# Attention output: the residual halves of the last two blocks are fetched ahead of the last four products

## The chip, the cores and the metric

One core of a Trainium2 chip runs the kernel in a single launch. The metric is device time in microseconds (us): 2112.7 us is the median of three runs before the change (2112.17 to 2113.65).

## The reference

The kernel computes a two-layer trunk on 1024 tokens of width 1024, in float32:

```python
for l in range(DEPTH):                       # DEPTH = 2
    if l < N_A:                              # layer 0
        h = h + recurrent_block(rmsnorm(h, a_norm[l]), ...)
    else:                                    # layer 1
        if l == N_A:
            k_pad, v_pad = shared_kv(h, kv_norm, w_kv, k_norm)
        q = rmsnorm((rmsnorm(h, b_norm[j]) @ b_w_q[j]).reshape(bsz, s, N_HEADS, HEAD_DIM), b_q_norm[j])
        o = chunk_band_attention(q, k_pad, v_pad, b_rel_bias[j])
        h = h + o @ b_w_o[j]                 # the change lies here
    h = h + sqrelu_mlp(rmsnorm(h, mlp_norm[l]), w_up[l], w_down[l])
```

`sqrelu_mlp(x) = square(relu(x @ w_up)) @ w_down`. The place of the change is `h + o @ b_w_o`: the product of the attention's output with its output weights, and the residual `h` that is added to it.

## The kernel before, in words

**Layout.** Activations lie transposed: 8 blocks of 128 features, each with 1024 tokens in two halves of 512 columns. Block `j`, half `h` is one tile of 128x512 floats (256 KB). A float32 product is made of three matmuls (L335 to L337, `mm`): each operand is split into a high part, copied by ScalarE in the reduced format, and a low part, the difference, made by VectorE. A product of one output tile has 8 blocks of input, so 24 matmuls of 512 columns.

**Attention output.** For output block `j` and half `h` TensorE sums the 24 matmuls in a PSUM bank. `Out.first` (L862) then fetches the residual tile from the DRAM tensor `x2d` into a buffer `s` of the pool `sp` (10 buffers, `sf()`), and VectorE adds bank and residual (L866) into `xr`. `Out.last` stores `xr` to the DRAM tensor `x3d`, since the MLP's last sum needs it again. Blocks 0 and 1 are made among the attention's own work. Blocks 2 to 5 are made by `Out.whole`, blocks 6 and 7 by `Out.end` in the order (6, 0), (7, 0), (6, 1), (7, 1), as (block, half).

**The MLP behind it.** The up product is one level of Strassen's scheme: seven products of sums of quarter matrices instead of eight. So the sums `xr` are themselves added, scaled by the norm's gains and split before TensorE can use them. For blocks 0 to 5 that is `Out.combine`, pair by pair. For blocks 6 and 7 it is the class `Begin`, which is written as chains of steps: `plain` and `mixed` wait for a flag `came[j, h]` that the residual sum sets, `square` and `lows` make the sum of squares for the norm, `sums` multiplies it with ones on TensorE (L366, L367), `outer` and `outer2` move the products out of PSUM (on ScalarE first: `c11`, `c22`), `loads` fetches the up weights of the second of 16 rounds. `mlp_up` then runs the rounds; in each the line L1356 makes the sum `c12` from a PSUM bank that TensorE's next product in that bank overwrites.

**What sets the order.** `end` and `Begin` stand in a region in which the program's own planner (`Plan`) steps the chains by estimated times and writes the instructions down in that order; each engine, and SyncE's queue, keeps it. Round 1 and later of `mlp_up` stand behind the region and are ordered by the framework's scheduler when the kernel is built. The same scheduler merges the region's first instructions with those of `whole` ahead of it. All DMAs here are issued by one engine, SyncE (SP), in order (`dma`, L244): one that has to wait holds those behind it.

Of the kernel before, what the change touches and what calls it, by code (L numbers as in the profile page):

```python
# [18 lines left out]
NF = 8  # L19
# [139 lines left out]
def tile_yoco_rglru_chunk_attention(  # L159
# [38 lines left out]
    def nm(s):  # L198
        cnt[0] += 1
        return f"{s}_{cnt[0]}"  # L200

    def gf(s="g"):
        return gp.tile([P, H2], F32, tag="g", name=nm(s))
# [4 lines left out]
    def sf(w=H2, s="s"):  # L208
        return sp.tile([P, w], F32, tag="s", name=nm(s))
# [22 lines left out]
    def bank(tag=None):  # L232
        if tag is None:
            tag = ("pj", "tp", "sc", "pj", "tp", "sc", "po", "sc")[ring[0] % 8]
            ring[0] += 1
        return ps1.tile([P, H2], F32, tag=tag, name=nm(tag), bufs=BANKS[tag])

    def hs(h):
        return slice(h * H2, (h + 1) * H2)
# [3 lines left out]
    def dma(dst, src):  # L243
        ins = nc.sync.dma_start(dst, src)  # L244
        if early[0]:
            early[0] -= 1
            tc.keep_in_program_order(ins)
# [91 lines left out]
    def mm3(ps, w, xs, half, span=None):  # L339
        n = len(xs)  # L340
        for k in range(n) if span is None else span:
            mm(ps, wparts(w, k), xs[k][half], k == 0, k == n - 1)
# [107 lines left out]
    def d_(n):  # L450
        return 0.16 + n * 0.00106
# [399 lines left out]
    class Out:  # L851
# [7 lines left out]
            self.XT = [[None] * 4 for _ in range(7)]  # L859
            self.rr = [None, None]  # L860

        def first(self, ps, j, h):  # L862
            xo = sf()
            dma(xo, self.resid[j, :, hs(h)])
            xt = gf("xr")
            dve.tensor_tensor(xt, ps, xo, ALU.add)  # L866
            self.XR[j][h] = xt
# [62 lines left out]
                    self.last(j, h)  # L930

        def end(self, Z, ws, plan, came):
            for h in range(2):
                for j in range(NF - 2, NF):
                    ps = bank()
                    for k in range(NF):
                        mm3(ps, ws[j], Z, h, (k,))
                        yield plan.pe(3 * H2) - LAT
                    self.first(ps, j, h)
                    came[j, h].set(plan.use("dve", d_(H2)))  # L940
                    self.last(j, h)

# [995 lines left out]
    for j in range(JP):  # L1938
        for h in range(2):
            ps = bank()  # L1940
# [80 lines left out]
```

## Time and profile before

| | before |
|---|---|
| median of three runs | 2112.7 us (2112.17 to 2113.65) |
| the profiled execution: run, span | 2111.56 us, 2109.8 us |
| granted TensorE clock, mean | 0.996 |
| TensorE busy | 2083.0 us (99%) |
| VectorE busy | 1564.0 us (74%) |
| ScalarE busy | 1104.0 us (52%) |
| GpSimd busy | 590.9 us (28%) |
| DMA | 319.19 MB, 151 GB/s in the mean |

The span runs from the first to the last instruction of the profiled execution; the run's time has some 1.8 us around it. In a row of the timeline the numbers are the start and the length in us; then engine, line of the kernel, operation, output `<-` inputs, shapes and count, and in brackets the engine's idle time before and what ended it. PE is TensorE, DVE VectorE, ACT ScalarE, POOL GpSimd, SPq SyncE's DMA queue. A row of waits reads: who waited for whom, total us, times, longest. The granted clock is the share of TensorE's full clock that was let through.

### The profile page before, as it was taken

To read this page: it belongs to the slowest core of one execution; us is meant where nothing else is said; L and a number is where in the kernel's file an instruction comes from. 1 tells how busy PE (TensorE), PEld (TensorE's weight loads), DVE (VectorE), ACT (ScalarE), POOL (GpSimd) and SP (SyncE) were. 2 spreads that over 40 slices of the span, in tenths; PEclk is the share of its full clock that TensorE was granted. 3 is DMA by queue.
4 is the path that set the end of the run, shared out by engine and by line. 5 is a ranking of instruction groups with operands and counts; after the bars stand their busy time and mean duration, and the time that the engine had idled before them with its cause. 6 is when DMAs were issued, how large, how long until landed. Compare 5 with 4: busy or idle time off the path is not lost.

```text
span 2109.8 us, 29361 instructions
## 1 busy us (share of the span) xinstructions
PE 2083.0 (99%) x9756; PEld 1729.7 (82%) x9756; DVE 1564.0 (74%) x2593; ACT 1104.0 (52%) x1965; POOL 590.9 (28%) x536
## 2 busy tenths in 40 slices
PE   9999999999999999999999999999899999999999
PEld 7788887888888888878888888878788888888887
DVE  8799869777777876557777777876877777777743
ACT  6878544344444454446666666764543434444631
POOL 2222104333300000047666666640233332000000
PEclk9999999999999999999999999999999999999999
DMA  4011436444488783523232233434444445987732
GB/s 163 30 51 58 160 101 209 150 154 149 156 316 278 229 256 118 160 83 100 81 94 86 77 88 99 121 119 133 158 162 150 150 151 193 327 260 245 237 107 93
DMA packets 174295, 319.19 MB, mean 151 GB/s; under 512 B 20544, under 2 KB 22592, under 8 KB 174144
## 3 DMA queue, kind: packets, MB, share of 16 engines
q1 hardware_dynamic: 174144, 317.33, 46.5%
q8 instruction: 76, 1.25, 0.3%
q14 instruction: 75, 0.61, 0.1%
HBM read 219.73 MB, written 78.64 MB: 141 GB/s over the span
## 4 chain that ended last, share of the span: by engine, by line
PE 91%; DVE 5%; DMA 1%; ACT 1%; issue 1%; SPq 0%; POOL 0%; DVEq 0%; ACTq 0%; POOLq 0%
PE pj L335 12%; PE pj L337 12%; PE pj L336 12%; PE tp L337 6%; PE tp L335 6%; PE tp L336 6%; PE sc L337 4%; PE sc L335 4%; PE sc L336 4%; PE p L336 4%; PE p L335 4%; PE p L337 4%; PE tp L1795 2%; PE po L1823 2%; PE po L1822 1%; PE sc L1770 1%
## 5 line engine op out<-in xcount | busy, mean ns | idle before, releaser
L335 PE MATMUL pj<-h,wh 128*128 128x512 f32 x1198 | 482.2, 403 | 3.4 <-DVE s L1356 2.4
L336 PE MATMUL pj<-l,wh 128*128 128x512 f32 x1198 | 468.7, 391 | 0.7 <-POOL l L1848 0.7
L337 PE MATMUL pj<-h,wl 128*128 128x512 f32 x1198 | 468.6, 391 | 0.0
L1066 ACT ACTIVATE wh<-raw 128x512 fp32r<-128x512 f32 x337 | 211.5, 630 | 325.1 <-PE po L336 82.7
L1067 DVE TENSOR_TENSOR wl<-raw,wh 128x512 fp32r<-128x512 f32 x337 | 270.0, 802 | 98.8 <-ACT wh L1066 94.9
L337 PEld LDWEIGHTS pj<-h,wl 128*128 128x128 f32 x1198 | 225.6, 188 | 48.9 <-DVE wl L1126 0.4
L335 PEld LDWEIGHTS pj<-h,wh 128*128 128x128 f32 x1198 | 226.3, 189 | 46.1 <-ACT wh L1066 2.6
L336 PEld LDWEIGHTS pj<-l,wh 128*128 128x128 f32 x1198 | 226.6, 189 | 39.5 <-POOL l L1848 1.4
L337 PE MATMUL tp<-h,wl 128*128 128x512 f32 x569 | 221.5, 389 | 1.4 <-DVE wl L1067 1.4
L335 PE MATMUL tp<-h,wh 128*128 128x512 f32 x569 | 221.5, 389 | 0.0
L336 PE MATMUL tp<-l,wh 128*128 128x512 f32 x569 | 221.4, 389 | 0.0
L349 DVE TENSOR_TENSOR l<-raw,h 128x512 fp32r<-128x512 f32 x224 | 153.5, 692 | 30.7 <-ACT h L348 29.4
L348 ACT ACTIVATE h<-raw 128x512 fp32r<-128x512 f32 x224 | 137.5, 620 | 55.4 <-DMA raw<-hid 32.6
L1327 ACT ACTIVATE s<-s 128x512 f32<-128x512 f32 x125 | 78.4, 629 | 166.4 <-DVE s L1326 166.3
L336 PE MATMUL sc<-l,wh 128*128 128x512 f32 x425 | 165.5, 389 | 0.0
L1075 POOL TENSOR_TENSOR raw<-raw,raw 128x512 f32<-128x512 f32 x30 | 49.9, 1664 | 412.4 <-DVE wl L1067 230.7
L337 PE MATMUL sc<-h,wl 128*128 128x512 f32 x425 | 165.2, 389 | 0.0
L335 PE MATMUL sc<-h,wh 128*128 128x512 f32 x425 | 165.2, 389 | 0.0
L335 PE MATMUL p<-h,wh 128*128 128x512 f32 x384 | 151.1, 394 | 1.6 <-ACT wh L493 1.5
L336 PE MATMUL p<-l,wh 128*128 128x512 f32 x384 | 150.3, 391 | 0.1
L337 PE MATMUL p<-h,wl 128*128 128x512 f32 x384 | 150.1, 391 | 0.0
L295 POOL TENSOR_TENSOR raw<-raw,vec 128x512 f32<-128x512 f32 x48 | 54.5, 1136 | 262.2 <-DMA raw<-in_w_kv 259.0
(302 smaller groups left out, 4235.8 us busy)
## 6 DMA issues: line engine op xcount, KB each, us to landing
raw<-hid SPq DMA_DIRECT2D x224, 256.0 KB, 3.6
hid<-s SPq DMA_DIRECT2D x221, 256.0 KB, 2.1
raw<-in_w_down SPq DMA_DIRECT2D x192, 256.0 KB, 3.5
raw<-in_w_up SPq DMA_DIRECT2D x128, 256.0 KB, 2.6
s<-in_w_down SPq DMA_DIRECT2D x64, 256.0 KB, 4.3
raw<-in_w_in SPq DMA_DIRECT2D x32, 256.0 KB, 2.7
raw<-in_w_kv SPq DMA_DIRECT2D x32, 256.0 KB, 3.4
od<-ev SPq DMA_DIRECT2D x48, 128.0 KB, 2.3
```

The lines of the kernel that those rows point to most:

```text
L295: pool.tensor_tensor(raw, raw, gains, ALU.mult)
L335: pe.matmul(ps, lhsT=wh, rhs=xh, start=start, stop=False, skip_group_check=more)
L336: pe.matmul(ps, lhsT=wh, rhs=xl, start=False, stop=False, skip_group_check=more)
L337: pe.matmul(ps, lhsT=wl, rhs=xh, start=False, stop=stop, skip_group_check=more)
L348: act.activation(h, src, AF.Copy)
L349: dve.tensor_tensor(l, src, h.bitcast(F32), ALU.subtract)
L1066: act.activation(wh, raw, AF.Copy)
L1067: dve.tensor_tensor(wl, raw, wh.bitcast(F32), ALU.subtract)
L1075: pool.tensor_tensor(raw[A11], raw[A11], raw[A21], ALU.add)
L1327: act.activation(out, out, AF.Square)
L1795: pe.transpose(pt[:, g * P : (g + 1) * P], sc[:, (kb - kb0) * P : (kb - kb0 + 1) * P], ident)
L1823: pe.matmul(out, lhsT=st, rhs=pl[:, off : off + wid], start=False, stop=y == final)
```

## The change

The four fetches of `Out.end` are issued at its start, in the order (6, 0), (7, 0), (6, 1), (7, 1), each into a buffer of its own; `first` takes the buffer when it is given one. Sums, stores and products are as they were.

```diff
-        def first(self, ps, j, h):
-            xo = sf()
-            dma(xo, self.resid[j, :, hs(h)])
+        def first(self, ps, j, h, xo=None):
+            if xo is None:
+                xo = sf()
+                dma(xo, self.resid[j, :, hs(h)])
             xt = gf("xr")
             dve.tensor_tensor(xt, ps, xo, ALU.add)
             self.XR[j][h] = xt
...
         def end(self, Z, ws, plan, came):
+            xo = {}
+            for h in range(2):
+                for j in range(NF - 2, NF):
+                    xo[j, h] = sf()
+                    dma(xo[j, h], self.resid[j, :, hs(h)])
             for h in range(2):
                 for j in range(NF - 2, NF):
                     ps = bank()
                     for k in range(NF):
                         mm3(ps, ws[j], Z, h, (k,))
                         yield plan.pe(3 * H2) - LAT
-                    self.first(ps, j, h)
+                    self.first(ps, j, h, xo[j, h])
                     came[j, h].set(plan.use("dve", d_(H2)))
                     self.last(j, h)
```

Six lines are added ahead of what follows, so the lines of `Begin` and `mlp_up` move by 6 (L1356 becomes L1362), the residual sum from L866 to L867.

The order moves at two places. On SyncE's queue, from the fetch of block 5's second half (`s_3736`) on, with the semaphores that each row waits for (those named DMAHW are of earlier DMAs on the same lane), before:

```order
L244 DMA s_3736_15208<-x2d_110 128x512 [waits DMAHW2_49]
L244 DMA x3d_111<-xr_3737_15210 128x512 [waits DMAHW3_49,DVE_49]
L244 DMA s_3764_15294<-x2d_110 128x512 [waits DMAHW4_49]
L244 DMA x3d_111<-xr_3765_15296 128x512 [waits DMAHW5_49,DVE_49]
L244 DMA s_3770_15331<-x2d_110 128x512 [waits DMAHW6_49]
L244 DMA x3d_111<-xr_3771_15333 128x512 [waits DMAHW7_49,DVE_49]
L244 DMA s_3775_15365<-x2d_110 128x512 [waits DMAHW0_49,Activation_49,Pool_49]
L244 DMA x3d_111<-xr_3776_15367 128x512 [waits DMAHW1_49,DVE_49]
L244 DMA s_3786_15410<-x2d_110 128x512 [waits DMAHW2_49,Activation_49]
L244 DMA x3d_111<-xr_3787_15412 128x512 [waits DMAHW3_49,DVE_49]
```

and with the change:

```order
L244 DMA s_3736_15208<-x2d_110 128x512 [waits DMAHW6_49]
L244 DMA x3d_111<-xr_3737_15210 128x512 [waits DMAHW7_49,DVE_49]
L244 DMA s_3759_15261<-x2d_110 128x512 [waits DMAHW0_49]
L244 DMA s_3760_15263<-x2d_110 128x512 [waits DMAHW1_49,Activation_49]
L244 DMA s_3761_15265<-x2d_110 128x512 [waits DMAHW2_49]
L244 DMA s_3762_15267<-x2d_110 128x512 [waits DMAHW3_49,Activation_49,Pool_49]
L244 DMA raw_3764_15273<-in_w_up 128x512 [waits DMAHW4_49]
L244 DMA raw_3765_15275<-in_w_up 128x512 [waits DMAHW5_49]
L244 DMA raw_3766_15277<-in_w_up 128x512 [waits DMAHW6_49]
L244 DMA raw_3767_15279<-in_w_up 128x512 [waits DMAHW7_49]
L244 DMA x3d_111<-xr_3768_15302 128x512 [waits DMAHW0_49,DVE_49]
L244 DMA x3d_111<-xr_3773_15337 128x512 [waits DMAHW1_49,DVE_49]
```

The stores (`x3d<-xr`) wait for VectorE's sum, and before the change a fetch stood behind each; now the four fetches stand together. The four loads of the second round's up weights (`in_w_up`), which stood among the fetches of blocks 3 to 5 before, now come behind them.

On VectorE, in the second round of the up product (the weight splits `wl`, and the sum of L1356), before:

```order
L1067 TENSOR_TENSOR wl_3843_15688<-raw_3760_15265,wh_3842_15687 128x512
L1067 TENSOR_TENSOR wl_3850_15733<-raw_3845_15724,wh_3849_15732 128x512
L1067 TENSOR_TENSOR wl_3852_15737<-raw_3846_15726,wh_3851_15736 128x512
L1067 TENSOR_TENSOR wl_3854_15741<-raw_3848_15730,wh_3853_15740 128x512
L1356 TENSOR_TENSOR s_3838_15679<-pj_3826_15584,s_3839_15680 128x512
L1067 TENSOR_TENSOR wl_3863_15805<-raw_3847_15728,wh_3862_15804 128x512
```

and with the change:

```order
L1073 TENSOR_TENSOR wl_3843_15688<-raw_3764_15273,wh_3842_15687 128x512
L1073 TENSOR_TENSOR wl_3850_15733<-raw_3845_15724,wh_3849_15732 128x512
L1073 TENSOR_TENSOR wl_3852_15737<-raw_3846_15726,wh_3851_15736 128x512
L1362 TENSOR_TENSOR s_3838_15679<-pj_3826_15584,s_3839_15680 128x512
L1073 TENSOR_TENSOR wl_3854_15741<-raw_3848_15730,wh_3853_15740 128x512
L1073 TENSOR_TENSOR wl_3863_15805<-raw_3847_15728,wh_3862_15804 128x512
```

The sum stands ahead of one weight split that it stood behind. TensorE's order is the same in both.

## The prediction

> **What bounds the kernel now.** I read the page's busy line first, then who TensorE waited for, then the chain of work that ended last around the place of the change.
>
> ```profile
> PE 2083.0 (99%) x9756; PEld 1729.7 (82%) x9756; DVE 1564.0 (74%) x2593; ACT 1104.0 (52%) x1965; POOL 590.9 (28%) x536
> ...
> PE po L366 <- ACT a L1122: 3.3, 1, 3.3
> ...
> PE pj L335 <- DVE s L1356: 2.4, 2, 2.2
> ...
> PE pj L335 <- DVE s L1362: 0.4, 1, 0.4
> ```
>
> The kernel is bound by TensorE (PE), busy 99% of the span. A wait row gives the total, the number of waits and the longest. The first lies just behind the four products of the change; the 2.2 of the second comes 30 us later. After 1530 us PE waits only 0.4 us (last row) to the end, so what is won before 1530 has nothing to hide behind. The chain says who sets the time between the two places (start, length, work):
>
> ```profile
> 1492.34 0.25 PE tp L337
> ...
> 1493.23 0.68 DVE wl L1126
> ...
> 1524.08 1.75 DVE wl L1067
> ...
> 1526.58 0.47 PE pj L335
> ```
>
> From 1492.6 to 1526.4 the path is VectorE (DVE), nearly without a gap; PE only joins again at 1526.58. DVE enters that stretch with the last residual sum. So the question is when that sum starts.
>
> ```profile
> 1479.10 0.69 DVE L352 SCALAR_TENSOR_TENSOR l<-s,h 128x512 fp32r<-128x512 f32 x1
> 1479.70 0.69 DVE L866 TENSOR_TENSOR xr<-tp,s 128x512 f32<-128x512 f32 x1
> 1481.24 0.75 DVE L1130 SCALAR_TENSOR_TENSOR l<-xr,vec,h 128x512 fp32r<-128x512 f32 x1 [0.85 <-ACT h L1122]
> 1481.91 0.69 DVE L1126 TENSOR_TENSOR acc<-acc,s 128x512 f32<-128x512 f32 x1
> 1484.08 0.69 DVE L866 TENSOR_TENSOR xr<-sc,s 128x512 f32<-128x512 f32 x1 [1.49 <-DMA s<-x2d]
> 1485.62 0.75 DVE L1130 SCALAR_TENSOR_TENSOR l<-xr,vec,h 128x512 fp32r<-128x512 f32 x1 [0.84 <-ACT h L1122]
> 1488.00 0.69 DVE L866 TENSOR_TENSOR xr<-po,s 128x512 f32<-128x512 f32 x1 [1.64 <-DMA s<-x2d]
> 1489.48 0.75 DVE L1130 SCALAR_TENSOR_TENSOR s<-xr,vec,s 128x512 f32<-128x512 f32 x1 [0.79 <-ACT s L1122]
> 1491.00 0.69 DVE L1126 TENSOR_TENSOR l<-s,h 128x512 fp32r<-128x512 f32 x1 [0.76 <-ACT h L1122]
> 1492.62 0.69 DVE L866 TENSOR_TENSOR xr<-sc,s 128x512 f32<-128x512 f32 x1 [0.93 <-PE tp L337]
> ```
>
> L866 is the residual sum; its four rows are (block 6, half 0), (7, 0), (6, 1), (7, 1). The brackets give idle time and releaser. The first sum follows other DVE work at once; the next two wait for the residual fetch. The last is put down to PE, but its product, the fourth of the four, was long done:
>
> ```profile
> 1484.01 0.39 PE L337 MATMUL sc<-h,wl 128*128 128x512 f32 x1
> ...
> 1480.42 0.32 SPq L244 DMA_DIRECT2D x3d<-xr  x1
> 1480.79 1.07 SPq L244 DMA_DIRECT2D s<-x2d  x1
> 1484.80 0.32 SPq L244 DMA_DIRECT2D x3d<-xr  x1
> 1485.22 0.37 SPq L244 DMA_DIRECT2D s<-x2d  x1
> ...
> 1489.13 0.38 SPq L244 DMA_DIRECT2D s<-x2d  x1
> ...
> DMA to landing us min/median/max: 2.0/2.7/5.7
> ```
>
> The fourth product ends at 1484.4, 8 us ahead of its sum. The fetch was issued at 1489.13, and about 3 us later (1492.6) it is there: the 0.93 is a DMA wait too. Each fetch stands on SyncE's (SP's) queue behind the store of the block before, and the store waits for that block's sum: sum, store, fetch, 3 us, sum.
>
> **The change part by part.** Nothing is computed anew: the same four fetches, sums and stores. (a) Three fetches leave the loop of sum, store and fetch. Before, (7,0) could be issued only behind the store at 1480.42. Now all four stand behind the store of block 5, and that one went out at 1470.88:
>
> ```profile
> 1470.88 0.32 SPq L244 DMA_DIRECT2D x3d<-xr  x1
> 1471.26 0.42 SPq L244 DMA_DIRECT2D s<-x2d  x1
> ```
>
> At 0.42 us each the last is issued at 1472.6. The worst landing above, 5.7 us, belongs to a burst of the stage before, so by the worst row all are there at 1478.3, ahead of the first sum (1479.70). What could hold them is their buffers. The fourth now waits for ScalarE and GpSimd, but in the program before the third fetch has the same two waits and went out at 1485.22, 0.1 us behind the store (1484.80 + 0.32): no price.
>
> The DVE steps then follow each other without DMA waits. Queued steps start 0.60 us apart (1479.10, 1479.70). Sum (7,0): 1481.91 + 0.60 = 1482.51. From a sum to the split behind it 1.54 (1484.08 to 1485.62): 1484.05. Sum (6,1), 0.67 behind (1481.24 to 1481.91): 1484.72. From there to the L1126 step 3.00 (1488.00 to 1491.00): 1487.72. Sum (7,1): 1488.32 in place of 1492.62. **4.30 us**, of which 4.06 are the three waits (1.49 + 1.64 + 0.93); the rest is queueing that overlaps. The fourth product (1484.4) is no limit.
>
> (b) PE's stall behind the products.
>
> ```profile
> 1492.18 0.40 PE L337 MATMUL tp<-h,wl 128*128 128x512 f32 x1
> 1495.89 0.50 PE L366 MATMUL po<-a,onesr 128*128 128x512 f32 x1 [3.31 <-ACT a L1122]
> 1497.03 0.79 PE L367 MATMUL po<-a,onesr 128*128 128x512 f32 x1 [0.65 <-DVE a L1126]
> 1498.02 0.80 PE L335 MATMUL pj<-h,wh 128*128 128x512 f32 x1 [0.20 <-ACT s L1122]
> ...
> 1500.61 0.39 PE L335 MATMUL pj<-h,wh 128*128 128x512 f32 x1
> 1500.84 0.39 PE L336 MATMUL pj<-l,wh 128*128 128x512 f32 x1
> ...
> 1497.00:1500.40 3.40, 3.17 (x7) 2.19 (x8) 3.40 (x6) 2.95 (x6) 0.00 (x0) 0.50 0.29 77
> ...
> 1527.80:1531.10 3.30, 3.30 (x9) 2.55 (x8) 3.15 (x4) 0.75 (x2) 1.13 (x1) 0.50 0.38 93
> ```
>
> The two rows by window end in granted clock, DMA share and GB/s. All that releases these three hangs on the last sum. 4.30 earlier, L366 is ready at 1491.59, so PE runs it as soon as it is free (1492.4); L367 at 1492.73; L335 at 1493.72. The stall shrinks to some 0.9 us and PE is 4.30 ahead. It also no longer enters a half clock (0.50): the six matmuls from 1498.02 to 1500.61 took 2.59 us; at 0.23 apart (1500.61 to 1500.84, the clock full again) they take 1.38, so 1.21 more. PE is then 5.51 ahead.
>
> (c) The next meeting point, 1526.58. PE's product there overwrites what the L1356 step reads. PE's last matmul before it starts at 1523.98; 5.51 earlier it is done at 1518.7. DVE's chain is 4.30 ahead, and one step has moved: the L1356 row now stands ahead of one weight split (the row at 1524.08, 1.67 us to the next start). 1525.75 - 4.30 - 1.67 = 1519.78; PE followed its start by 0.83: 1520.61. 1526.58 - 1520.61 = **5.97 us**. PE waits some 1.9 us there, as before (2.21), so the half clock behind it (1.65 of the 3.30 us at 0.50) stays.
>
> (d) One round later.
>
> ```profile
> 1525.75 0.68 DVE L1356 TENSOR_TENSOR s<-pj,s 128x512 f32<-128x512 f32 x1
> ...
> 1544.89 0.69 DVE L1356 TENSOR_TENSOR s<-pj,s 128x512 f32<-128x512 f32 x1 [0.37 <-issue]
> ...
> 1547.36 0.39 PE L335 MATMUL pj<-h,wh 128*128 128x512 f32 x1
> ...
> 1563.93 0.69 DVE L1356 TENSOR_TENSOR s<-pj,s 128x512 f32<-128x512 f32 x1 [0.94 <-PE pj L337]
> ```
>
> DVE could have been at the second L1356 at 1544.52; 4.30 earlier and 0.83 for PE gives 1541.05, 6.3 ahead of 1547.36. So no more than 6.3 passes here whatever PE wins before, and 5.97 passes. From the round after that on (1563.93) DVE waits for PE here, and the end follows PE.
>
> (e) The four loads of up weights in the same region now stand behind the fetches: issued by about 1474.4 (eight issues of 0.4 from 1471.26), landed by the worst row at 1480.1, and copied by ScalarE first here:
>
> ```profile
> 1501.04 0.63 ACT L1122 ACTIVATE wh<-raw 128x512 fp32r<-128x512 f32 x1
> ```
>
> 4.30 earlier that is 1496.7, so there are 16 us in hand. No price.
>
> The sum: 2109.8 - 6.0 = 2103.8 us of span. The run of that profile took 2111.56, the median of the runs shown is 2112.7, 1.14 more; I take 6.0 off the median: **2106.7 us**. Bounds: 4.3 if the moved step gives nothing; 6.3 by (d), beyond which up to 9.4 (5.51 + 2.21 + 1.65) if DVE's own stretch got shorter too.
>
> The half clock deserves care. Here waits of 2.21 and 3.31 us were followed by 0.50. The Trainium skill (TensorE: Matmul & The Clock Gate, "What's actually happening") says that the clock falls after an idle window of about 3.4 us. By that rule a wait of 1.9 us at 1518.7 would leave the clock full, and PE would be 5.97 + 1.65 ahead until (d) caps it: 2106.4. The trace speaks against it, since 2.21 sufficed; I keep 2106.7.
>
> **The rivals.** *The moved step gives nothing* (20%): L1362, as it is called now, waits for something else, or the splits ahead stretch. Then DVE's 4.30 is all: 2112.7 - 4.3 = 2108.4. For it: the chain there has steps of 1.5 to 1.75 where others take 0.60, so their length is not steady. Against it: the order is fixed at build.
>
> *More than the sum* (8%): DVE's stretch shortens as its steps meet GpSimd's otherwise, the second wait goes too. 2112.7 - 9.4 = 2103.3 at most.
>
> *Hidden* (12%): the sums find another wait, such as ScalarE's copies in line behind them (they take 0.8 each in the rows above), or DVE loses elsewhere what it gained, so that 0 to 3.5 is left: about 2111. Against it: the sums' only waits are fetch and product, and the products are done.
>
> *Slower* (5%): the up weights, now queued behind four fetches on SP, come late for the product after the stall. That decides only if they land after 1496.7, where ScalarE copies them; each us beyond costs PE one. To lose what is won they must land after 1502.7, 28 us behind their issue, against 5.7 as the worst of a fetch; at 33 us the time would be 2117. Only a buffer that comes free late could do it.
>
> **How the numbers follow.** The forecast case, 5 to 6.6 us, has 55%, the rivals 20, 8, 12 and 5. A measurement of this kernel tells about 0.2%, 4.2 us, from no change. Faster by over that: 55 + 8 + half of the 20, whose value lies on the line = 73%; within: 10 + 12 = 22%; slower 5%. For 8 in 10 I take 2104.5 to 2110.2: the forecast, the moved-step rival and a part of the next two. The likeliest case alone spans 2106.1 to 2107.7.
>
> **What would show it.** L867's waits for x2d gone in the last three sums, the last one near 1488.3; four x2d issues in a row behind 1470.9; L366's wait of 3.3 gone and no 0.50 clock at 1493 to 1497; PE's wait on L1362 (now c12's first sum) at 1519 to 1521. Wrong would be: a fetch issued late, or a last sum near 1488 with PE still resuming past 1524.

## The result and the profile after

The changed kernel takes **2101.86 us** (median of six runs, 2098.96 to 2102.58) beside 2112.7 us for the kernel before in six runs taken with them: a ratio of 0.9947, 95% interval 0.9934 to 0.9959. A second measurement of both programs gave 2102.53 beside 2110.78 us (ratio 0.9959, 0.9946 to 0.9971; five and 27 runs). The change is worth 8 to 11 us. I had forecast 6.0, and 2106.7 us; the time lies below the range.

The profiled execution of after took 2100.08 us, its span is 2098.3 us. First TensorE's busy line and its waits (total, times, longest), as they were shown of before:

```profile
PE 2077.5 (99%) x9756; PEld 1725.9 (82%) x9756; DVE 1559.2 (74%) x2593; ACT 1102.6 (53%) x1965; POOL 593.2 (28%) x536
...
PE pj L335 <- DVE s L1368: 1.5, 2, 1.1
...
PE pj L335 <- ACT s L1128: 0.5, 1, 0.5
PE pj L335 <- DVE s L1362: 0.4, 2, 0.3
```

The wait of 3.3 us behind the four products is down to 0.5, as forecast. But the wait of 2.2 us for the sum of round 1 (L1356 before, L1362 now), which I had left standing, is gone too. What is left on that line is 0.3 one round later (at 1535.77) and 0.2 in the first layer's MLP (at 350.89), which before has too. The two waits on L1368 have nothing to do with the change: 1.1 stands in the first layer's MLP at 603.86, where the kernel before with small GpSimd adds, shown below, has 0.9; and 0.4 stands at 1788, where the first profile of before has the same 0.4 (its L1362).

The timeline of after around the change: SyncE's queue, the four residual sums, and where TensorE resumes.

```profile
1468.40 0.32 SPq L244 DMA_DIRECT2D x3d<-xr  x1
1468.77 1.87 SPq L244 DMA_DIRECT2D s<-x2d  x4
1470.69 2.36 SPq L244 DMA_DIRECT2D raw<-in_w_up  x4
1477.93 0.33 SPq L244 DMA_DIRECT2D x3d<-xr  x1
...
1477.22 0.68 DVE L867 TENSOR_TENSOR xr<-tp,s 128x512 f32<-128x512 f32 x1
1480.03 0.69 DVE L867 TENSOR_TENSOR xr<-sc,s 128x512 f32<-128x512 f32 x1
1482.22 0.69 DVE L867 TENSOR_TENSOR xr<-po,s 128x512 f32<-128x512 f32 x1
1485.82 0.69 DVE L867 TENSOR_TENSOR xr<-sc,s 128x512 f32<-128x512 f32 x1
...
1491.22 0.50 PE L335 MATMUL pj<-h,wh 128*128 128x512 f32 x1 [0.49 <-ACT s L1128]
```

The four fetches go out together behind the store of block 5, no sum waits for one, and the last sum is 8.60 us behind the first (1485.82 - 1477.22) in place of 12.92 (1492.62 - 1479.70). That is 4.32 us won; the prediction had 4.30.

The two profiles differ by 2.5 us before the change is reached (the first sum is at 1477.22 against 1479.70). So all dates below are counted from a row that every program here has ahead of the place, TensorE's matmul that waits some 0.27 us for ScalarE at 1412.06 us before and at 1409.79 after (in us, "stretch" is VectorE's time from the last residual sum to the sum of round 1):

| from the row at 1412 / 1409 to | before | before, again | after | after, again |
|---|---|---|---|---|
| last residual sum | 80.56 | 80.54 | 76.03 | 75.88 |
| TensorE resumes behind the products | 85.96 | 85.95 | 81.43 | 81.28 |
| TensorE's product behind the sum of round 1 | 114.52 | 115.37 | 106.52 | 106.35 |
| the end of the span | 697.74 | 696.38 | 688.51 | 687.93 |
| VectorE's stretch | 33.13 | 34.01 | 28.89 | 28.89 |

At the end after is 8.8 us ahead (means of the two columns each). 4.6 us of it are there when TensorE resumes, the rest comes in the 30 us behind that: VectorE's stretch became 4.24 us shorter in the first pair and 5.12 in the second, where I had counted 1.67 for the step that changed its place. These rows show why. GpSimd adds weight quarters there (L1075 to L1080 before, L1081 to L1086 after); first before:

```profile
1503.86 2.27 POOL L1075 TENSOR_TENSOR raw<-raw,raw 128x512 f32<-128x512 f32 x1 [89.75 <-DMA s<-in_w_down]
1506.21 1.74 POOL L1076 TENSOR_TENSOR raw<-raw,raw 128x512 f32<-128x512 f32 x1
1506.72 1.79 DVE L1130 SCALAR_TENSOR_TENSOR rneg<-s,rneg 128x512 f32<-128x512 f32 x1
1511.44 2.38 DVE L1326 SCALAR_TENSOR_TENSOR s<-s,rneg 128x512 f32<-128x512 f32 x2
1511.65 1.62 POOL L1078 TENSOR_TENSOR raw<-raw,raw 128x512 f32<-128x512 f32 x1 [3.69 <-issue]
1513.74 1.77 DVE L1067 TENSOR_TENSOR wl<-raw,wh 128x512 fp32r<-128x512 f32 x1
...
1520.85 1.39 DVE L1067 TENSOR_TENSOR wl<-raw,wh 128x512 fp32r<-128x512 f32 x2
1522.32 1.29 POOL L1075 TENSOR_TENSOR raw<-raw,raw 128x512 f32<-128x512 f32 x1 [7.35 <-DVE wl L1067]
1522.55 3.28 DVE L1067 TENSOR_TENSOR wl<-raw,wh 128x512 fp32r<-128x512 f32 x2 [0.31 <-ACT wh L1066]
1523.68 1.59 POOL L1076 TENSOR_TENSOR raw<-raw,raw 128x512 f32<-128x512 f32 x1
```

and after:

```profile
1497.06 2.27 POOL L1081 TENSOR_TENSOR raw<-raw,raw 128x512 f32<-128x512 f32 x1 [85.23 <-DMA s<-in_w_down]
1499.41 2.33 POOL L1082 TENSOR_TENSOR raw<-raw,raw 128x512 f32<-128x512 f32 x1
1499.88 0.70 DVE L1136 SCALAR_TENSOR_TENSOR rneg<-s,rneg 128x512 f32<-128x512 f32 x1
...
1506.62 1.62 POOL L1086 TENSOR_TENSOR raw<-raw,raw 128x512 f32<-128x512 f32 x1
1507.24 1.56 DVE L1073 TENSOR_TENSOR wl<-raw,wh 128x512 fp32r<-128x512 f32 x1
...
1513.50 1.29 DVE L1073 TENSOR_TENSOR wl<-raw,wh 128x512 fp32r<-128x512 f32 x2 [0.50 <-ACT wh L1072]
1514.27 1.67 POOL L1081 TENSOR_TENSOR raw<-raw,raw 128x512 f32<-128x512 f32 x1 [6.03 <-DVE wl L1073]
1514.71 0.69 DVE L1362 TENSOR_TENSOR s<-pj,s 128x512 f32<-128x512 f32 x1
...
1516.31 0.39 PE L335 MATMUL pj<-h,wh 128*128 128x512 f32 x1
```

The same `rneg` step takes 1.79 us beside GpSimd's add before and 0.70 after, and there the add takes 2.33 in place of 1.74: in each of these pairs one of the two is held up by the other. The two splits ahead of L1356 took 3.28 us together, beside two adds; now the sum L1362 stands ahead of one of them, and the add at 1514.27 runs beside the sum, which reads PSUM and takes its 0.69. The sum is done before TensorE wants its bank, and TensorE runs into the product at 1516.31 with no wait. The Trainium skill (SBUF — State Buffer, "Who interferes with whom") says that a VectorE step with two SBUF inputs contends with a GpSimd step that reads SBUF, for a port pair that only one of them can hold, that the order of issue decides who is blocked, and that a VectorE step with at most one SBUF input, outside the two-port modes, does not contend; the rows above agree, with 1.56 to 1.79 against 0.70 us for the held steps and 0.69 for the sum out of PSUM.

### The profile page after: what moved, and what is told of

Same layout as the page of the kernel before. It is cut to its first block, busy times and chain, and to the rows that moved or that the text cites. A ratio compares the mean times of both kernels' runs of the same rounds, so it can differ in the third digit from the quotient of the medians.

```text
span 2098.3 us, 29355 instructions
## 1 busy us (share of the span) xinstructions
PE 2077.5 (99%) x9756; PEld 1725.9 (82%) x9756; DVE 1559.2 (74%) x2593; ACT 1102.6 (53%) x1965; POOL 593.2 (28%) x536
## 4 chain that ended last, share of the span: by engine, by line
PE 87%; DVE 6%; DMA 3%; issue 2%; ACT 2%; POOL 0%; SPq 0%; DVEq 0%; POOLq 0%; ACTq 0%
PE pj L335 11%; PE pj L336 11%; PE pj L337 11%; PE tp L337 6%; PE tp L335 6%; PE tp L336 6%; PE p L336 4%; PE p L337 4%; PE p L335 4%; PE sc L336 4%; PE sc L335 4%; PE sc L337 4%; PE tp L1801 2%; PE po L1829 2%; PE po L1828 1%
## 5 line engine op out<-in xcount | busy, mean ns | idle before, releaser
L1081 POOL TENSOR_TENSOR raw<-raw,raw 128x512 f32<-128x512 f32 x30 | 50.3, 1678 | 403.3 <-DVE wl L1073 226.2
```

Source lines behind the costliest of these rows:

```text
L1081: pool.tensor_tensor(raw[A11], raw[A11], raw[A21], ALU.add)
```

## The experiments

### Both programs once more

Copies with a comment added.

> The kernel before, once more, for the noise and for a second profile. 2.5 us of the 11.5 us between the two profiles lie ahead of the change (the sum of block 6 starts at 1479.70 before and 1477.22 after), some 1.7 of it in a bout of half clock at 1391 to 1394.7, behind a wait of TensorE of 1.9 us that both programs have. 'Chance': the bout belongs to the run, not to the kernel; this profile may show it or not, and the time stays within 2112.7 +- 1.5. 'The change did it': the bout and the 2.5 us are here again as in the kernel before, and not in the next run. Either way the wait of 3.3 us behind the four products and the one of 2.2 us in round 1 come back at the same offsets from the sum of block 6 (18.3 us and 46.9 us).

> The changed kernel, once more: 2101.9 +- 1.5 us. 'Chance' for the 2.5 us ahead of the change: this profile may have the half clock at 1391, and then the sum of block 6 is near 1479 and the time is up to 2.5 us longer than in the other runs. Both theories on the change: the last residual sum 8.6 us behind the first of the four (1485.82 - 1477.22), no wait of TensorE on the sum of round 1 over 0.5 us, no half clock behind the four products.

Measured: 2111.23 us (11 runs) and 2102.53 (5). The table above has the second profiles. The 2.5 us ahead of the change were chance: after, run again, has its first sum at 1479.95, as late as before, and without half clock near 1390, so that date moves by more than the one bout. In the first profile of before a half clock followed TensorE's wait of 1.90 us at 1389.93, in the second profile of before, with a wait of 1.98 us at the same place, it did not. The windows just behind that wait end in granted clock, DMA share and GB/s; first before, then before again:

```profile
1391.00:1394.40 3.40, 3.40 (x17) 3.17 (x16) 0.95 (x3) 2.11 (x5) 3.40 (x5) 0.53 0.00 0
```

```profile
1391.80:1395.20 3.40, 3.40 (x25) 3.05 (x25) 1.79 (x4) 2.84 (x7) 3.40 (x5) 1.00 0.00 0
...
1496.20:1499.60 3.40, 3.21 (x7) 2.22 (x8) 3.40 (x6) 2.95 (x6) 0.00 (x0) 0.50 0.28 77
1526.60:1529.90 3.30, 3.30 (x15) 2.74 (x16) 3.15 (x3) 1.27 (x2) 2.28 (x2) 1.00 0.24 75
```

The other two windows of before again stand behind the four products and behind the sum of round 1. The wait of 3.3 us brings half clock again, and for twice as long: the granted clock is at 0.50 from 1497.0 to 1500.4 in the first profile, 3.4 us, and from 1495.0 to 1501.9 in the second, 6.8 us. The wait of 1.94 us in round 1 does not this time, where 2.21 us did in the first profile. So the bout in round 1 that the prediction let "stay" is there in some executions of before and not in others, and the bout behind the products is there each time.

### The last residual sum late again

```diff
+                    if (j, h) == (NF - 1, 1):
+                        for _ in range(6):            # 3 in the second run
+                            dve.tensor_tensor(xo[j, h], xo[j, h], xo[j, h], ALU.max)
                     self.first(ps, j, h, xo[j, h])
```

All other instructions keep the order of after, on every engine.

> After, with six VectorE steps in place (each tile written over itself, values unchanged) ahead of the last residual sum, so that this sum is as late as before the change, by 6 x 0.60 to 0.75 = 3.6 to 4.5 us; the order of everything else is that of after. It separates the date of the last sum from the changed order in round 1. 'Chain' (time follows the last sum one to one): 2101.9 + 4.2 = 2106.1, or 2107.3 with the half clock behind TensorE's wait. 'Order and chain' (my prediction's sum): only the moved step of 1.67 stays won, 2112.7 - 1.7 = 2111.0. 'Meeting' (VectorE's stretch of 33 us is longer or shorter by how its steps meet GpSimd's, which start by other dates): anything up to 2112.7, with the wait on the sum of round 1 back at 0.5 to 2.2 us and VectorE's steps of 1.5 to 2.4 us among GpSimd's adds.

> After with three of the six VectorE steps ahead of the last residual sum, half the dose: the sum 2.2 us later. Six of them gave 2108.7, 6.1 us over after, for 4.42 us of delay. 'Chain', one to one: 2102.5 + 2.2 = 2104.7. 'Threshold' (TensorE's wait behind the products is 0.4 in after and 3.1 with six; with three it is about 2.6 - the half clock of 1.2 us follows if a wait of that size lets the clock fall): 2105.9. 'Meeting by chance of dates': GpSimd's adds meet other VectorE steps at this date, the stretch from the last sum to the sum of round 1 is anything between 28.9 (after) and 30.9 us (with six): 2104.7 to 2107.

Measured: 2108.67 us with six steps (ratio to before 0.9988, 0.9979 to 0.9997) and 2104.75 with three (five runs, 2102.18 to 2105.72). From the same row as in the table:

| | last sum | TensorE resumes | product of round 1 | end | stretch |
|---|---|---|---|---|---|
| after | 76.03 | 81.43 | 106.52 | 688.51 | 28.89 |
| three steps | 77.94 | 83.35 | 108.46 | 689.99 | 28.89 |
| six steps | 80.27 | 85.68 | 112.42 | 694.42 | 30.87 |
| before | 80.56 | 85.96 | 114.52 | 697.74 | 33.13 |

The first 1.9 us of delay cost 1.9 at the product, and 2.2 in the median against after again. The next 2.3 cost 4.0 at the product: TensorE takes 26.74 us from resuming to the product in place of 25.11, since its wait is now long enough for half clock. The timeline of the run with three steps, and the window from its second wait on:

```profile
1493.92 0.50 PE L366 MATMUL po<-a,onesr 128*128 128x512 f32 x1 [0.74 <-ACT a L1131]
1495.07 0.49 PE L367 MATMUL po<-a,onesr 128*128 128x512 f32 x1 [0.64 <-DVE a L1135]
1496.06 0.50 PE L335 MATMUL pj<-h,wh 128*128 128x512 f32 x1 [0.49 <-ACT s L1131]
```

```profile
1495.00:1498.40 3.40, 2.84 (x11) 2.12 (x12) 3.40 (x7) 2.95 (x7) 0.00 (x0) 1.00 0.28 77
```

and the same with six:

```profile
1487.73 4.32 DVE L947 TENSOR_TENSOR s<-s 128x512 f32<-128x512 f32 x6
1492.15 0.69 DVE L867 TENSOR_TENSOR xr<-sc,s 128x512 f32<-128x512 f32 x1
...
1495.42 0.80 PE L366 MATMUL po<-a,onesr 128*128 128x512 f32 x1 [3.06 <-ACT a L1131]
1497.56 0.80 PE L335 MATMUL pj<-h,wh 128*128 128x512 f32 x1 [0.19 <-ACT s L1131]
```

```profile
1496.60:1500.00 3.40, 3.21 (x7) 2.21 (x8) 3.40 (x6) 2.95 (x6) 0.00 (x0) 0.50 0.32 77
```

Three waits of 0.5 to 0.7 us leave the clock at 1.00, one of 3.06 brings 0.50. With six steps the last sum is as late as before (80.27 against 80.56), and still 2.1 us are won against 2110.78 (0.6 to 4.4 by the interval of the ratio): that is the order of round 1 without the earlier sum. There is no wait for the sum of round 1 in that run, though the half clock is there. 'Chain' alone, 2106.1 or 2107.3, missed by 1.4 to 2.6 us; my 2111.0 missed by 2.3 on the other side. 'Meeting' had that wait back at 0.5 to 2.2 us: it stayed away, though VectorE does have steps of 1.78 us, and 2.39 for two, beside GpSimd's adds. With three steps 'chain' had 2104.7; 'threshold' supposed a wait of some 2.6 us, and the longest is 0.74.

### GpSimd's adds made small

The adds keep their place and their order, but do 16 of 512 columns in rounds 1 and 2 of the second layer; in the kernel before and in after.

```diff
-        pool.tensor_tensor(raw[A11], raw[A11], raw[A21], ALU.add)
+        pool.tensor_tensor(raw[A11][:, :n], raw[A11][:, :n], raw[A21][:, :n], ALU.add)
...
-                s1, s2 = up_sums(raw)
+                s1, s2 = up_sums(raw, 16 if layer == 1 and q < 3 else H2)
```

> The kernel before, with GpSimd's four adds of weight quarters in rounds 1 and 2 of the second layer's up product done on 16 of 512 columns (so the sums of weights are wrong in the rest); the order on every engine is that of before. 'Meeting' (GpSimd's adds lengthen VectorE's steps between 1492 and 1526, by 1.79 - 0.6, 2.38 - 0.6, 1.77 - 0.6, 1.53 - 0.6 and 1.67 - 0.6, some 6 us): VectorE reaches the sum of round 1 before TensorE wants it, the 2.2 us wait and the half clock of 1.65 us behind it go: 2112.7 - 3.9 = 2108.8, and up to 0.4 us more by the next round. Rival (these steps are long by themselves, or wait for ScalarE's copies): steps as long as before, 2112.7.

> After, with GpSimd's four adds of weight quarters in rounds 1 and 2 of the second layer's up product done on 16 of 512 columns, as in the run of the kernel before with small adds (2107.8); the sums of weights are wrong in the rest. It asks what the change is worth where GpSimd's adds lengthen nothing. 'Chain': 4.4 of the last residual sum and 1.2 of the half clock behind the stall, 2107.8 - 5.6 = 2102.2, and against after (2102.5) no difference, since TensorE no longer waits for the sum of round 1 there. 'Meeting carries most of the gain': less than 4 us between the two kernels with small adds, so above 2103.8.

Measured: 2107.8 us for before with small adds (0.9982, 0.9974 to 0.9991), 3.0 under 2110.78 where 3.9 was forecast, and 2102.12 for after with them. VectorE's stretch in before falls from 33.13 to 29.94 us, and TensorE no longer waits for the sum of round 1: the rows of that kernel ahead of the sum, beside the 1.39 and 3.28 us of the same two rows above.

```profile
1520.87 1.39 DVE L1067 TENSOR_TENSOR wl<-raw,wh 128x512 fp32r<-128x512 f32 x2
1522.58 1.32 DVE L1067 TENSOR_TENSOR wl<-raw,wh 128x512 fp32r<-128x512 f32 x2 [0.31 <-ACT wh L1066]
1523.90 0.69 DVE L1356 TENSOR_TENSOR s<-pj,s 128x512 f32<-128x512 f32 x1
...
1522.34 0.22 POOL L1075 TENSOR_TENSOR raw<-raw,raw 128x16 f32<-128x16 f32 x1 [7.58 <-DVE wl L1067]
1522.64 0.71 POOL L1076 TENSOR_TENSOR raw<-raw,raw 128x16 f32<-128x16 f32 x1
```

The two splits take 1.32 us in place of 3.28, in the same order. So the wait of 2.2 us in before was GpSimd's doing; before again, whose half clock behind the products is as long as here (6.8 us), waits 1.94 us with whole adds. The 29.94 us are no longer VectorE's own length: on the way it waits for TensorE (0.49, 0.20 and 0.75 us), which that half clock has made late. In after the small adds change nothing that can be told (2102.12 against 2102.53), since TensorE does not wait for the sum of round 1 there. Between the two kernels with small adds 5.7 us are left of the change (5.6 forecast for it): the last sum and the half clock behind the products. The other 2 to 3 us of the change are GpSimd's adds no longer being waited for.

### The last sum late, with small adds

Six steps as above, and small adds.

> After with the last residual sum 4.4 us later, and small GpSimd adds. The sum 4.4 later gave 6.1 to 6.4 us (2108.7), of which TensorE's rows put 4.4 on the sum and 1.64 on half clock between its resuming and the product of round 1 (26.74 us in place of 25.10). 'Half clock': the same with small adds, 2102.1 + 4.4 + 1.6 = 2108.1. 'Meeting' (the 2 us that VectorE's stretch is longer are GpSimd's, and reach the end): 2102.1 + 4.4 = 2106.5.

Measured: 2107.67 us. 'Half clock' had 2108.1, 'meeting' 2106.5; with runs from 2104.37 to 2109.84 the time alone hardly tells them apart, TensorE's rows do. It needs 27.65 us from resuming to the product of round 1, against 25.09 in after with small adds, and waits for no sum there. VectorE's stretch is longer too, 30.53 us against 27.97, with no long add beside it: VectorE waits for TensorE's banks (0.97, 0.32, 0.69, 0.36 and 0.27 us). So what the second half of the delay costs beyond its length is half clock on TensorE, not VectorE's longer stretch.

### The loads of the up weights first

```diff
-            self.raw = [wload(w_up[self.layer, 1, x]) for x in range(4)]     # in Begin.loads
+            self.raw = [wload(w_up[self.layer, 1, x]) for x in range(4)]     # at the top of Begin.start
```

> After, with the four loads of the second round's up weights issued ahead of the residual fetches, where the scheduler spreads them among the fetches of blocks 3 to 5 as before the change; the order on the four compute engines is that of after. My term (e) priced the later loads at nothing: then 2102.5 +- 0.5. Rival (loads or fetches that stand together collide, or the later weights hold the splits): up to 1 us faster than after, with the ScalarE copies of these weights earlier; or slower, if the four fetches now come late: each us that the first sum waits shows at the end.

Measured: 2102.11 us, and 688.22 us from the row of the table to the end, against 688.51 and 687.93 of after. The loads' place has no price that can be told (0.4 us under after again, in runs from 2100.79 to 2105.88), as term (e) had it.

### More fetches ahead

In `Out.whole`, the residual of the next tile is fetched ahead of the sum of this one; in a second kernel only that of its last tile, (5, 1), and in a third all of them, with GpSimd's small adds.

```diff
                     mm3(ps, w, Z, h)
-                    self.first(ps, j, h)
+                    get(n + 1)                         # xo[next] = sf(); dma(xo[next], self.resid[next])
+                    n += 1
+                    self.first(ps, j, h, xo[j, h])
```

> After, and in the blocks before the last two the residual half of the next tile is fetched ahead of the sum of the one before it too. VectorE waits there 8.3 us for such fetches in after (five waits). 'Chain goes on': the first of the last four sums comes earlier, what is left of TensorE's waits behind it (0.5 behind the products, 0.3 and 1.1 in round 2) goes: 2102.5 - 1 to 2 = 2100.5 to 2101.5. 'No path there': TensorE is the bound ahead of the last four products, the sums are not waited for, and only VectorE's idle time moves: 2102.5. 'Meeting': the order that the scheduler gives in rounds 1 and 2 changes with it, and GpSimd's adds meet other steps: up to 2 us slower.

> After, and of the blocks before only the fetch for the last tile, (5, 1), one tile earlier: VectorE is ahead at the first of the last four sums by the 1.7 us that it waits there in after, no more. 'Chain goes on': TensorE's 0.5 us behind the products goes, 2102.3 - 0.5 = 2101.8. 'Meeting': the dates of VectorE's steps against GpSimd's adds differ from those of after, 2101.8 to 2104.2; the wait for the sum of round 1 comes back as in the run with all fetches ahead.

> The kernel with all residual fetches of blocks 2 to 7 one tile ahead (2104.2, with TensorE's wait for the sum of round 1 back at 2.4 us), and GpSimd's adds of rounds 1 and 2 done on 16 of 512 columns (the sums of weights are wrong in the rest); the order on the other engines is the same. 'Meeting' (that wait comes from splits on VectorE of 1.0, 3.2 and 1.1 us beside GpSimd's adds): the wait goes, and the half clock that some runs have behind it: 2101 to 2102. Rival (the wait comes from the order that the scheduler gave, so from the splits ahead of the sum by their number): 2104.2 as before, the wait still over 1.5 us.

Measured: 2104.23, 2103.92 and 2101.24 us. The first expectation counted a wait of 1.1 us in round 2 that stands in the first layer (at 603.86), so no more than 0.5 and 0.3 us were there to win. With all fetches ahead the last sum comes 3.7 us earlier than in after (72.36), TensorE resumes with no wait, 0.66 us earlier, and then stands for 2.42 us on the sum of round 1:

```profile
1512.04 0.68 DVE L1086 TENSOR_TENSOR wl<-raw,wh 128x512 fp32r<-128x512 f32 x1
1513.07 1.36 DVE L1086 TENSOR_TENSOR wl<-raw,wh 128x512 fp32r<-128x512 f32 x1 [0.34 <-ACT wh L1085]
1516.27 1.20 DVE L1086 TENSOR_TENSOR wl<-raw,wh 128x512 fp32r<-128x512 f32 x1 [1.84 <-ACT wh L1085]
1517.39 0.68 DVE L1375 TENSOR_TENSOR s<-pj,s 128x512 f32<-128x512 f32 x1
...
1511.60 2.27 POOL L1094 TENSOR_TENSOR raw<-raw,raw 128x512 f32<-128x512 f32 x1 [7.85 <-DVE wl L1086]
1513.95 1.62 POOL L1095 TENSOR_TENSOR raw<-raw,raw 128x512 f32<-128x512 f32 x1
1515.61 0.63 ACT L1085 ACTIVATE wh<-raw 128x512 fp32r<-128x512 f32 x1 [2.57 <-POOL raw L1095]
...
1518.21 0.47 PE L335 MATMUL pj<-h,wh 128*128 128x512 f32 x1 [2.42 <-DVE s L1375]
```

With the fetch of (5, 1) alone it is the same, 2.43 us. The scheduler has put two more splits ahead of the sum than in after, and the second, at 1516.27, is the split of a sum that GpSimd makes: VectorE waits 1.84 us for ScalarE, ScalarE 2.57 for GpSimd. With small adds, in the same order, the wait is gone and the kernel is 3.0 us faster, as 'meeting' had it. 'Chain goes on' (2100.5 to 2101.5, and 2101.8) did not come true. The rival that counted only the splits fell too: they stand ahead of the sum and cost nothing when GpSimd is quick. No kernel that computes the whole reference beat after by more than can be told.

## Why the prediction was wrong, point by point

**(a), right.** 4.30 us forecast, 4.32 measured, and the three waits for x2d are gone. The whole of it reaches TensorE's resuming (85.96 to 81.43 is 4.5; the other 0.2 lies ahead of the first sum). The steps between the sums follow at the distances that were forecast: 2.81, 5.00 and 8.60 us behind the first, against 2.81, 5.02 and 8.62.

**(b), right in kind, with a half clock that was sized from one profile.** The stall was to shrink to some 0.9 us, it is 0.5, and no half clock follows. I priced the half clock at 1.21 us. 28.56 us from resuming to the product in the first profile of before, less the 2.21 us of waiting and the 25.09 of after, is 1.26; the second profile gives 29.42 - 1.94 - 25.09 = 2.39, and the run with six steps 1.65. The granted clock says why: in the profile that I read the half clock lasts 3.4 us, in the four other profiles with a wait of over 3 us at this place 6.8 us. Half of the part that lies behind TensorE's resuming is 1.2 us in the first profile of before and 2.4 in the second, near the 1.26 and 2.39 above. The 1.21 fitted the profile that it was taken from, and not the kernel.

**(c), the step that failed.** "PE waits some 1.9 us there, as before (2.21), so the half clock behind it (1.65 of the 3.30 us at 0.50) stays." I let VectorE's stretch keep its length but for one step of 1.67 us. It fell by 4.24 in the first pair of profiles and 5.12 in the second, and TensorE did not wait at all. Two causes are separated by the run with six steps, which has the order of after and the late sum of before. The order: 4.90 us from the last four splits to the sum of round 1 in before (1520.85 to 1525.75) became 2.39 for three (1512.32 to 1514.71), 2.51 in place of 1.67, because the sum out of PSUM now stands where GpSimd's adds held a split up. The rest, 1.7 to 2.6 us, comes earlier in the stretch. In the first profile of before GpSimd's adds hold up VectorE there three times by some 1.1 us (the steps of 1.79, 2.38 for two, and 1.77), in after by some 1.3 us in all (steps of 0.86 and 1.56). This rest goes with the half clock: with the order of after and whole adds the stretch is 28.88 or 28.89 in all four profiles without half clock behind the products, and 30.87 in the one with it. That the half clock shifts the dates at which VectorE and GpSimd meet is argued and not shown: VectorE waits 0.18 us for TensorE's bank in that run and 0.69 in the second profile of before, but not in the first, and no run changes the clock alone. The runs with small adds show that the half clock also lengthens the stretch without GpSimd (30.53 against 27.97), by VectorE's waits for TensorE.

The rows for it were in the profile before. I had quoted the long steps (1.5 to 1.75 where others take 0.60) as "not steady" and used them as a reason for less gain. GpSimd's rows beside them would have told who held them: small adds take 3.2 us out of the 33.1.

**(d), wrong by the same step.** The cap of 6.3 us one round later rested on VectorE's second L1356 at 1544.52, less the 4.30 us. In after it starts at 1535.04, and 9.3 us of lead pass there (135.30 to 125.98), 8.7 in the second pair. (In the first pair the half clock of round 1, 1.65 us, is part of it.) Some 0.6 to 1.0 us are given back behind the product: from there to the end it is 581.99 and 581.58 us in after, 581.01 in the second profile of before. TensorE's wait on L1362 one round later is 0.3 of that (0.27 and 0.30 us); where the rest goes stays open.

**(e), right**, as far as the run with the loads first can tell.

**The rivals.** "More than the sum" named the mechanism that came true (VectorE's steps meet GpSimd's otherwise, the second wait goes too) with up to 9.4 us and 2103.3, and got 8%. "The moved step gives nothing" was refuted: the order alone is worth 2.1 us. "Hidden" and "slower" had no part in it.

**The base.** The three runs of before that were shown, 2112.17 to 2113.65, lie high: 27 more have a median of 2110.78 and a spread from 2107.81 to 2114.31, and two later sets, of nine and 15, have 2110.33 and 2110.55. Against that base the change is worth 8.3 us, and the account closes at the product of round 1: 4.5 + 1.3 + 2.2 = 8.0 in the first pair of profiles, 4.7 + 2.4 + 1.9 = 9.0 in the second (resuming, half clock, wait). The bout in round 1 adds 1.65 in the executions that have it.

## What to carry to other kernels

When a chain on one engine is shortened, price the stretch behind it anew, row by row: a step that is longer than its kind is held up by somebody, and that changes with every date and with the order. Here the place of one sum against another engine's adds was worth 2.1 us by the medians, half of the waits that the change took away (4.06), and with either sign: two kernels that fetched even earlier came out 1.4 to 2.4 us slower by theirs. A wait long enough to bring half clock cost its length and the bout here; shortening it below that is worth more than the microseconds taken away (2.3 us of delay cost 4.0).

## What was not expected of the hardware

A half clock behind a wait of TensorE does not follow from the length of the wait alone. In the 13 profiles here it follows the wait behind the four products whenever that is 3.06 us or more (five of five), and never a wait of 0.74 or less at that place. In between it goes either way: in round 1 it followed 2.21 us, not 1.94, 2.42 or 2.43 us; at the place at 1390, with waits of 1.64 to 2.01 us in every profile, it came in six of 13, behind none of the five waits up to 1.84 us and behind six of the eight from 1.89 us on. At these places it lasted 3.4 or 6.8 us, nothing between. The Trainium skill (TensorE: Matmul & The Clock Gate, "What's actually happening") has a free-running window of 3.4 us, which fits that one wait falls either way in two executions; that a window has to be idle does not fit, since 1.9 and 2.21 us were enough. Bouts that cost 1.3 to 2.6 us each, there or not, are also of the size by which the runs of one program differ here.
